# Second feed-forward products of phases one and two as seven block products, sums kept in DRAM

## The chip, the cores and the metric

The kernel runs on one core of one Trainium2 chip. The metric is the device time of one execution in microseconds (us). Three runs of the kernel before gave 1245.04, 1245.33 and 1245.99 us, median 1245.33.

## What is computed

A decoder trunk of two layers on 512 tokens of width 1024, all float32. Each layer is a mixer (layer 0: gated linear recurrence and retention; layer 1: sparse attention) and a SwiGLU feed-forward part of hidden width 2816, both behind an RMS norm and added to the residual:

```
def swiglu(x, w1, w3, w2):
    return (jax.nn.silu(x @ w1) * (x @ w3)) @ w2
...
for layer in range(DEPTH):
    hn = rmsnorm(h, attn_norm[layer])
    ...
    h = h + swiglu(rmsnorm(h, ffn_norm[layer]), ffn_w1[layer], ffn_w3[layer], ffn_w2[layer])
return rmsnorm(h, final_norm)
```

The change is in the feed-forward part, which runs once per layer, so twice.

## The kernel before, in words

Each float32 product is made of three passes at the fast matmul rate: an operand is split into a rounded high part and the rest (`mm3`, lines 196 to 203: high by high on L201, then the two mixed passes on L202 and L203). Weights come from DRAM in pieces of at most 1 MB into one of four `wr` buffers (SyncE's queue, L117). ScalarE casts a half of such a piece into `whi` (L136, two instructions), and VectorE makes `wlo` (L137). `prefetch` (L180) keeps this at most four parts of 1024 columns ahead of the matmuls; `whi` and `wlo` have four buffers each.

The residual `h` is held feature-major: two tiles of 128 partitions by 4 by 512 tokens. The feed-forward part (`ffn`, L702) walks the hidden width in three phases `ph` of 1024, 1024 and 768 columns. A phase has two first products, `q` = 0 and 1 (512 hidden columns each, 384 in the third phase), and then the second product:

- A first product gives w1 and w3 at once by `strassen` (L275): seven block products instead of eight, called here by their place `j` = 0 to 6 and by the PSUM tile they use (X, Y, V, V, X, X, Z). Each has 2 row blocks by 4 terms by 3 passes, 24 matmuls. The weight operands that are sums of blocks are formed by DMA: `plan_set` (L151) loads three blocks and adds others onto them with an accumulating DMA issued by GpSimd (L161), eight of them per set of weights. `keep` (L284) copies a PSUM result to an SBUF tile `part`, `add` (L288) adds a later one to it. The result is token-major (tokens on partitions). SiLU and the product with the other half follow (L735, L741), then four TensorE transposes per token block (`turn`, L723, L726) and the split into `gh` and `gl` (L729, L730), feature-major.
- The second product takes w2 as weights and `gh`, `gl` as the moving side (L761 to L801): eight output blocks `m` of 128 features, each with 8 terms by 3 passes of 512 columns in phases one and two. `done` (L765) adds the PSUM tile to `h` (L767). Its weights are plain loads, four pieces of 1 MB a phase (`w2a`, `w2c`), each split once.

Every engine runs its own queue in order. The instructions of a queue are ordered ahead of time from the program text and priorities, and semaphores do the rest. GpSimd's queue holds the accumulating DMAs in this part of the program, SyncE's queue the plain DMAs. Pools: `big` has 13 buffers of 8 KB per partition (seven hold the first products' operands, two `h`, four `gh` and `gl`), `gr` 12 buffers of 2 KB.

Of the kernel before, what the change touches and what calls it, by code (L numbers as in the profile page):

```python
# [17 lines left out]
F32 = mybir.dt.float32  # L18
# [45 lines left out]
class Trunk:  # L64
# [210 lines left out]
    def strassen(self, sg, n, after, last):  # L275
# [8 lines left out]
        def keep(b, name, i, r):  # L284
            c = rest[name, i] = self.g2([P, S], name="part")[:, 0:n]
            A.activation(c, ps[b, i][:, 0:n], AF.Copy, scale=r())

        def add(b, name, i, r):  # L288
            c = rest.pop((name, i))
            V.scalar_tensor_tensor(c, ps[b, i][:, 0:n], r(), c, op0=ALU.mult, op1=ALU.add)  # L290
            after(name, i, c)
        R = lambda t: (lambda: self.rtok[:, t:t + 1])
        N = lambda t: (lambda: self.ntok[:, t:t + 1])
        for j, (b, op) in enumerate((("X", "A11"), ("Y", "A12"), ("V", "S1"), ("V", "S4"), ("X", "S2"), ("X", "S3"), ("Z", "A22"))):
            last(j)
            if j == 1:
                for i in range(2):
                    keep("X", "11", i, R(i))
            first = j in (0, 1, 2, 6)
            for i in range(2):  # L300
                if first:
                    ps[b, i] = self.psA("ps_" + b) if b in "XV" else self.psB("ps_" + b)
                o = ps[b, i][:, 0:n]
                self.mm3(o, [self.sg_at(sg, op, p, slice(i * P, (i + 1) * P)) + w.at((j * 4 + p) * n, (j * 4 + p + 1) * n) for p in range(4)], first, True, j in (3, 4, 5))
                if j == 1:
                    add("Y", "11", i, R(i))
                elif j == 2:
                    keep("V", "22", i, R(2 + i))
                elif j == 3:
                    keep("V", "12", i, R(i))  # L310
                elif j == 4:
                    add("X", "12", i, N(i))
                elif j == 5:
                    add("X", "22", i, N(2 + i))
                    keep("X", "21", i, R(2 + i))
                elif j == 6:
                    add("Z", "21", i, R(2 + i))
# [366 lines left out]
    def plan_ffn(self, layer):  # L684
        for ph in range(3):
            for j in range(2):
                if ph < 2:
                    self.plan_set("wff%d" % layer, (2 * ph + j,), 2048)
                else:
                    self.plan_set("wfg%d" % layer, (j,), 1536)  # L690
            for j in range(2):
                if ph < 2:
                    self.plan("w2a%d" % layer, 2 * ph + j, 2048)
                else:
                    self.plan("w2b%d" % layer, j, 1536)
            for j in range(2):
                if ph < 2:
                    self.plan("w2c%d" % layer, 2 * ph + j, 2048)
                else:
                    self.plan("w2d%d" % layer, j, 1536, 768)  # L700

    def ffn(self, layer, sg, gain_next, want_hg=True):  # L702
# [10 lines left out]

        for ph in range(3):
            gs = []
            for q in range(2):
                n = S if ph < 2 else 3 * P
                nj = n // P
                g = [self.b8([P, 4, S], F32R, name="g" + x) for x in "hl"]
# [3 lines left out]
                def turn(t, v, g=g, nj=nj):  # L723
# [3 lines left out]
                    p4 = pt[:, 0:nj * P].rearrange("p (j c) -> p j c", j=nj)  # L727
                    hi, lo = (x[:, 0:nj, t * P:(t + 1) * P] for x in g)
# [15 lines left out]
                def before(j):  # L744
# [4 lines left out]
                    flush(j)  # L749

                flush(7)
                later[:] = [(j - 7, f) for j, f in later]
                self.strassen(sg, n, after, before)
# [20 lines left out]
            flush(7)  # L774
            w = [self.unit(), self.unit()]
# [36 lines left out]
        return hn  # L812

# [545 lines left out]
def pack(i):  # L1359
# [28 lines left out]
    for l in range(2):  # L1388
# [8 lines left out]
        o["w2a%d" % l] = c(np.stack([w2u((4 * q, 4 * q + 4), (0, 4)) for q in range(4)]))  # L1397
        o["w2b%d" % l] = c(np.stack([w2u((16 + 3 * q, 19 + 3 * q), (0, 4)) for q in range(2)]))
        o["w2c%d" % l] = c(np.stack([w2u((8 * ph, 8 * ph + 8), (4 + 2 * q, 6 + 2 * q)) for ph in range(2) for q in range(2)]))
# [28 lines left out]
```

## Time and profile before

| | |
|---|---|
| median of three runs | 1245.33 us |
| the profiled execution, time and span | 1245.73 us, 1243.8 us |
| TensorE matmul busy | 1221.5 us, 98% of the span |
| VectorE, ScalarE, GpSimd busy | 799.1, 686.3, 232.0 us |
| granted TensorE clock | 0.996 of full speed |
| the chain that ended last | PE 88%, ACT 5%, DVE 4% |
| DMA bytes | 149.23 MB, 120 GB/s on average |

A matmul's row shows about 0.39 us from its start to its modelled end, but the next starts after 0.23 us: what counts is the distance between starts. The same holds for short instructions on ScalarE and VectorE, whose starts follow each other some 0.1 us closer than the rows' durations say.

### The profile page before, as it was taken

What the parts mean: (1) busy time and instruction counts of PE and PEld (TensorE: products, weight loads), DVE (VectorE), ACT (ScalarE), POOL (GpSimd) and SP (SyncE); (2) the same over time, 40 slices, a digit from 0 to 9 for tenths busy, and PEclk for the clock granted to TensorE, in tenths of its full rate; (3) what the DMA queues carried; (4) which work ended last, traced back from release to release, by engine and by line L of the source; (5) the groups of instructions that cost most, each with busy time, mean ns of one, the idle gap of its engine ahead of it and who ended that gap; (6) DMA issues with size and microseconds to landing.
All of it is one profiled execution on the core that took longest, in us unless ns stands there. A gap on an engine that the chain in (4) does not pass through costs nothing.

```text
span 1243.8 us, 16442 instructions
## 1 busy us (share of the span) xinstructions
PE 1221.5 (98%) x6077; PEld 1031.4 (83%) x6077; DVE 799.1 (64%) x1237; ACT 686.3 (55%) x1395; POOL 232.0 (19%) x303
## 2 busy tenths in 40 slices
PE   9999999999999999999999999999999999999997
PEld 7688888888888889988888878877888888888996
DVE  6886629666356636674364889986776537653764
ACT  6541447664256426655454688995666336633653
POOL 0001420220012002100000568680111011101200
PEclk9999999999999999999999999999999999999998
DMA  9122143784388328852100000134488358824832
GB/s 342 68 102 68 35 169 102 172 191 150 98 191 178 138 64 182 228 194 71 66 35 1 1 1 1 35 113 159 108 197 186 120 120 185 201 82 106 181 93 68
DMA packets 35535, 149.23 MB, mean 120 GB/s; under 512 B 3936, under 2 KB 6256, under 8 KB 26624
## 3 DMA queue, kind: packets, MB, share of 16 engines
q1 hardware_dynamic: 21296, 100.88, 22.8%
q0 software_dynamic: 14016, 47.27, 21.4%
q8 instruction: 48, 0.79, 0.2%
q14 instruction: 31, 0.25, 0.1%
q10 hardware_dynamic: 144, 0.04, 0.0%
HBM read 143.98 MB, written 4.19 MB: 119 GB/s over the span
## 4 chain that ended last, share of the span: by engine, by line
PE 88%; ACT 5%; DVE 4%; POOL 1%; issue 1%; DMA 0%; POOLq 0%; DVEq 0%; SPq 0%; ACTq 0%
PE ps L203 6%; PE ps L201 6%; PE ps L202 6%; PE ps_t L201 5%; PE ps_X L201 5%; PE ps_X L203 5%; PE ps_X L202 5%; PE ps_t L203 5%; PE ps_t L202 5%; PE ps_V L201 3%; PE ps_V L203 3%; PE ps_V L202 3%; ACT prob L1175 2%; PE ps_Y L201 2%; PE ps_Z L203 2%; PE ps_Z L201 2%
## 5 line engine op out<-in xcount | busy, mean ns | idle before, releaser
L136 ACT CAST whi<-wr 128x512 fp32r<-128x512 f32 (+1 forms) x540 | 295.1, 593 | 348.1 <-PE ps L202 126.2
L137 DVE TENSOR_TENSOR wlo<-wr,whi 128x1024 fp32r<-128x1024 f32 (+2 forms) x272 | 313.3, 1154 | 208.9 <-ACT whi L136 205.4
L201 PE MATMUL ps<-gh,whi 128*128 128x512 f32 (+1 forms) x364 | 139.8, 384 | 0.0
L203 PE MATMUL ps<-gh,wlo 128*128 128x512 f32 (+1 forms) x364 | 139.2, 382 | 0.0
L202 PE MATMUL ps<-gl,whi 128*128 128x512 f32 (+1 forms) x364 | 139.1, 382 | 0.0
L161 POOL DMA_DIRECT2D wr<-wff x64 | 55.6, 868 | 366.8 <-DVE wlo L137 327.8
L201 PE MATMUL ps_t<-whi,hgh 128*128 128x512 f32 x288 | 114.7, 399 | 0.0
L202 PE MATMUL ps_t<-wlo,hgh 128*128 128x512 f32 x288 | 113.3, 394 | 0.0
L203 PE MATMUL ps_t<-whi,hgl 128*128 128x512 f32 x288 | 112.7, 391 | 0.0
L201 PE MATMUL ps_X<-whi,sg 128*128 128x512 f32 (+1 forms) x288 | 107.2, 372 | 0.0
L203 PE MATMUL ps_X<-whi,sg 128*128 128x512 f32 (+1 forms) x288 | 106.9, 371 | 0.0
L202 PE MATMUL ps_X<-wlo,sg 128*128 128x512 f32 (+1 forms) x288 | 106.8, 371 | 0.0
L1185 POOL TENSOR_TENSOR prob<-prob,rs 128x384 f32<-128x384 f32 (+3 forms) x128 | 88.1, 722 | 1.9
L767 DVE TENSOR_TENSOR h<-ps,h 128x512 f32<-128x512 f32 x46 | 31.8, 691 | 82.6 <-PE ps L203 82.6
L203 PEld LDWEIGHTS ps<-gh,wlo 128*128 128x128 f32 x364 | 68.4, 188 | 13.3
L202 PEld LDWEIGHTS ps<-gl,whi 128*128 128x128 f32 x364 | 68.4, 188 | 13.2
L201 PEld LDWEIGHTS ps<-gh,whi 128*128 128x128 f32 x364 | 68.4, 188 | 13.0
L1175 ACT ACTIVATE prob<-ps_s,nm 128x384 f32<-128x384 f32 (+3 forms) x128 | 68.2, 540 | 15.8 <-DVE nm L1171 14.9
L201 PE MATMUL ps_V<-whi,sg 128*128 128x512 f32 (+1 forms) x192 | 71.2, 371 | 0.0
L202 PE MATMUL ps_V<-wlo,sg 128*128 128x512 f32 (+1 forms) x192 | 71.2, 371 | 0.0
L203 PE MATMUL ps_V<-whi,sg 128*128 128x512 f32 (+1 forms) x192 | 71.2, 371 | 0.0
L203 PEld LDWEIGHTS ps_t<-whi,hgl 128*128 128x128 f32 x288 | 54.1, 188 | 11.5 <-issue 0.2
(316 smaller groups left out, 2568.6 us busy)
## 6 DMA issues: line engine op xcount, KB each, us to landing
wr<-wff POOLq DMA_DIRECT2D x64, 512.0 KB, 5.9
wr<-wff SPq DMA_DIRECT2D x24, 1024.0 KB, 4.8
wr<-wfg POOLq DMA_DIRECT2D x32, 384.0 KB, 5.8
wr<-w0t SPq DMA_DIRECT2D x10, 1024.0 KB, 5.9
wr<-w1t SPq DMA_DIRECT2D x10, 1024.0 KB, 4.9
wr<-wfg SPq DMA_DIRECT2D x12, 768.0 KB, 4.3
wr<-w2a SPq DMA_DIRECT2D x8, 1024.0 KB, 4.8
wr<-w2c SPq DMA_DIRECT2D x8, 1024.0 KB, 5.0
```

What stands on the lines that cost most here:

```text
L136: self.nc.scalar.copy(hi[:, c], x[:, c])
L137: self.nc.vector.tensor_tensor(lo, x, hi.bitcast(F32), op=ALU.subtract)
L161: self.nc.gpsimd.dma_start(x[:, c], more[:, c], accum_op=ALU.add)
L201: mm(ps, ah, bh, start=(first and k == 0), stop=False)
L202: mm(ps, ah, bl, start=False, stop=False)
L203: mm(ps, al, bh, start=False, stop=(last and k == n - 1))
L767: V.tensor_tensor(hm, ps, hm, op=ALU.add)
L1175: A.activation(u.p[:, r, b, 0:u.nk], u.ps[:, b, :], AF.Exp, bias=u.nm[:, b:b + 1], accum_out=u.rs[:, r, b:b + 1])
L1185: Q.tensor_tensor(x, x, u.rs[:, r, b:b + 1].broadcast_to([P, u.nk]), op=ALU.mult)
```

## The change

The second products of phases one and two now also go by `strassen`, with the hidden values as the stationary side and w2 as the moving side, so that their results are token-major. The first products of these phases leave the hidden values unsplit in one tile `g` each. A new function `second` forms from them the seven left operands `gop` (A11, A12, S1, S4, S2, S3, A22; four of them sums or differences of quarters, made in place on VectorE), each split into high part (ScalarE, L856 of the changed kernel) and rest (VectorE, L857), one product ahead of its use; two buffers of the pool `big` are left for them. `strassen` gets these operands through a function and without scale factors. w2 comes by `plan_set` as a set of four blocks `w2s`. Each finished sum of 128 tokens by 512 features is written to the DRAM tensor `sums` (L888). In the third phase the sum of phase one is read back (L775), that of phase two is added by an accumulating DMA (L776), and `turned` transposes it (four TensorE transposes of 128 by 128) and adds it to `h`; one of the eight sums is turned ahead of each of the block products 1 to 6 of the third phase's first first product, and 1 and 2 of its second. The third phase's own second product is unchanged.

```diff
@@ -272,7 +272,8 @@
         for i, w in ((0, u), (2, v)):
             put(*(sg[2][z][p // 2][:, p % 2, i:i + 2] for z in range(2)), w)
-    def strassen(self, sg, n, after, last):
+    def strassen(self, opnd, n, after, last, scaled=True):
         nc = self.nc
@@ -283,11 +284,17 @@
         def keep(b, name, i, r):
             c = rest[name, i] = self.g2([P, S], name="part")[:, 0:n]
-            A.activation(c, ps[b, i][:, 0:n], AF.Copy, scale=r())
-
-        def add(b, name, i, r):
+            if scaled:
+                A.activation(c, ps[b, i][:, 0:n], AF.Copy, scale=r())
+            else:
+                A.copy(c, ps[b, i][:, 0:n])
+        def add(b, name, i, r, sub=False):
             c = rest.pop((name, i))
-            V.scalar_tensor_tensor(c, ps[b, i][:, 0:n], r(), c, op0=ALU.mult, op1=ALU.add)
+            if scaled:
+                V.scalar_tensor_tensor(c, ps[b, i][:, 0:n], r(), c, op0=ALU.mult, op1=ALU.add)
+            else:
+                V.tensor_tensor(c, c, ps[b, i][:, 0:n], op=ALU.subtract if sub else ALU.add)
             after(name, i, c)
         R = lambda t: (lambda: self.rtok[:, t:t + 1])
         N = lambda t: (lambda: self.ntok[:, t:t + 1])
@@ -301,7 +308,7 @@
                 if first:
                     ps[b, i] = self.psA("ps_" + b) if b in "XV" else self.psB("ps_" + b)
                 o = ps[b, i][:, 0:n]
-                self.mm3(o, [self.sg_at(sg, op, p, slice(i * P, (i + 1) * P)) + w.at((j * 4 + p) * n, (j * 4 + p + 1) * n) for p in range(4)], first, True, j in (3, 4, 5))
+                self.mm3(o, [opnd(op, p, slice(i * P, (i + 1) * P)) + w.at((j * 4 + p) * n, (j * 4 + p + 1) * n) for p in range(4)], first, True, j in (3, 4, 5))
                 if j == 1:
                     add("Y", "11", i, R(i))
                 elif j == 2:
@@ -309,9 +316,9 @@
                 elif j == 3:
                     keep("V", "12", i, R(i))
                 elif j == 4:
-                    add("X", "12", i, N(i))
+                    add("X", "12", i, N(i), True)
                 elif j == 5:
-                    add("X", "22", i, N(2 + i))
+                    add("X", "22", i, N(2 + i), True)
                     keep("X", "21", i, R(2 + i))
                 elif j == 6:
                     add("Z", "21", i, R(2 + i))
@@ -688,16 +695,13 @@
                     self.plan_set("wff%d" % layer, (2 * ph + j,), 2048)
                 else:
                     self.plan_set("wfg%d" % layer, (j,), 1536)
+            if ph < 2:
+                self.plan_set("w2s%d" % layer, (ph,), 2048)
+                continue
             for j in range(2):
-                if ph < 2:
-                    self.plan("w2a%d" % layer, 2 * ph + j, 2048)
-                else:
-                    self.plan("w2b%d" % layer, j, 1536)
+                self.plan("w2b%d" % layer, j, 1536)
             for j in range(2):
-                if ph < 2:
-                    self.plan("w2c%d" % layer, 2 * ph + j, 2048)
-                else:
-                    self.plan("w2d%d" % layer, j, 1536, 768)
+                self.plan("w2d%d" % layer, j, 1536, 768)
     def ffn(self, layer, sg, gain_next, want_hg=True):
         nc = self.nc
@@ -711,12 +715,24 @@
             while later and later[0][0] <= j:
                 later.pop(0)[1]()
+        sums = self.dram.tile([2, NT, P, D], F32, name="sums%d" % layer)
+        back = []
+        def turned(t, c, tiles):
+            pt = self.psC("ps_tr")
+            for k in range(4):
+                T.transpose(pt[:, k * P:(k + 1) * P], tiles[:, k * P:(k + 1) * P], self.ident)
+            x = h[c][:, :, t * P:(t + 1) * P]
+            V.tensor_tensor(x, pt.rearrange("p (k s) -> p k s", k=4), x, op=ALU.add)
         for ph in range(3):
             gs = []
             for q in range(2):
                 n = S if ph < 2 else 3 * P
                 nj = n // P
-                g = [self.b8([P, 4, S], F32R, name="g" + x) for x in "hl"]
+                g = [self.b8([P, 4, S], F32R, name="g" + x) for x in "hl"] if ph == 2 else self.b8([P, 4, S], name="g")
                 gs.append((g, nj))
                 vals = {}
@@ -725,6 +741,9 @@
                     for j in range(nj):
                         T.transpose(pt[:, j * P:(j + 1) * P], v[:, j * P:(j + 1) * P], self.ident)
                     p4 = pt[:, 0:nj * P].rearrange("p (j c) -> p j c", j=nj)
+                    if nj == 4:
+                        A.copy(g[:, :, t * P:(t + 1) * P], p4)
+                        return
                     hi, lo = (x[:, 0:nj, t * P:(t + 1) * P] for x in g)
                     A.copy(hi, p4)
                     V.tensor_tensor(lo, p4, hi.bitcast(F32), op=ALU.subtract)
@@ -747,10 +766,19 @@
                         self.ntok = self.const.tile([P, NT], F32, tag="ntok", name="ntok", bufs=2)
                         V.tensor_scalar(self.ntok, self.rtok, -1.0, None, op0=ALU.mult)
                     flush(j)
+                    if j and back:
+                        turned(*back.pop(0))
+                    if ph == 2 and q == 0:
+                        for i in range(j + (j > 0), j + 2):
+                            x = self.g2([P, S], name="sum")
+                            src = [sums[u, i // 2, :, i % 2 * S:(i % 2 + 1) * S] for u in range(2)]
+                            nc.sync.dma_start(x, src[0])
+                            nc.gpsimd.dma_start(x, src[1], accum_op=ALU.add)
+                            back.append((i // 2, i % 2, x))
                 flush(7)
                 later[:] = [(j - 7, f) for j, f in later]
-                self.strassen(sg, n, after, before)
+                self.strassen(partial(self.sg_at, sg), n, after, before)
             if ph == 2 and want_hg:
                 self.load_gates()
                 hn = self.new_hg()
@@ -772,6 +800,9 @@
                     if not want_hg:
                         A.activation(hm, hm, AF.Copy, scale=self.gain[4][:, m:m + 1])
             flush(7)
+            if ph < 2:
+                self.second(gs[0][0], gs[1][0], sums[ph], flush)
+                continue
             w = [self.unit(), self.unit()]
             ps = [self.psA("ps_2") for _ in range(4)]
             nj = [gs[q][1] for q in range(2)]
@@ -810,6 +841,54 @@
         for _ in late:
             pass
         return hn
+    def second(self, g0, g1, dst, flush):
+        V, A = self.nc.vector, self.nc.scalar
+        a, b = slice(0, 256), slice(256, S)
+        src = {"A11": g0[:, :, a], "A12": g1[:, :, a], "S3": g0[:, :, b], "A22": g1[:, :, b], "S2": g0[:, :, a], "S4": g1[:, :, a]}
+        ops = {}
+        def make(n):
+            t = ops[n] = self.b8([P, 2, 4, 256], F32R, name="gop")
+            for c in (slice(0, 2), slice(2, 4)):
+                x = src[n][0 if c.start == 0 else 1] if n == "S1" else src[n][:, c]
+                A.copy(t[:, 0, c], x)
+                V.tensor_tensor(t[:, 1, c], x, t[:, 0, c].bitcast(F32), op=ALU.subtract)
+        def sums1():
+            src["S1"] = []
+            for c in (slice(0, 2), slice(2, 4)):
+                x = self.g2([P, 2, 256], name="s1")
+                V.tensor_tensor(x, g0[:, c, b], g1[:, c, b], op=ALU.subtract)
+                src["S1"].append(x)
+        def sums2():
+            for z, c in enumerate((slice(0, 2), slice(2, 4))):
+                V.tensor_tensor(g0[:, c, b], g0[:, c, a], g0[:, c, b], op=ALU.subtract)
+                V.tensor_tensor(g0[:, c, a], src["S1"][z], g0[:, c, a], op=ALU.subtract)
+                V.tensor_tensor(g1[:, c, a], g1[:, c, a], g0[:, c, a], op=ALU.add)
+        def before(j):
+            if j == 0:
+                make("A12")
+            elif j == 1:
+                flush(99)
+                sums1()
+                make("S1")
+                sums2()
+            elif j < 6:
+                make(("S4", "S2", "S3", "A22")[j - 2])
+        def after(name, i, c):
+            t = 2 * (name[0] == "2") + i
+            u = name[1] == "2"
+            self.nc.sync.dma_start(dst[t, :, u * S:(u + 1) * S], c)
+        make("A11")
+        self.strassen(lambda n, p, c: tuple(ops[n][:, z, p, c] for z in range(2)), S, after, before, False)
     def rope(self, x, n, cos, sin):
@@ -1394,9 +1473,10 @@
         t2 = w2.reshape(NH, P, 8, P)
         w2u = lambda j, m: t2[slice(*j)][:, :, slice(*m)].transpose(1, 2, 0, 3).reshape(P, -1)
-        o["w2a%d" % l] = c(np.stack([w2u((4 * q, 4 * q + 4), (0, 4)) for q in range(4)]))
+        half = lambda ph, z, u: w2[1024 * ph + 512 * z:1024 * ph + 512 * z + 512, 512 * u:512 * u + 512].reshape(4, P, 512).transpose(1, 0, 2).reshape(P, -1)
+        o["w2s%d" % l] = c(np.stack([np.stack([half(ph, z, u) for u in range(2) for z in range(2)]) for ph in range(2)]))
         o["w2b%d" % l] = c(np.stack([w2u((16 + 3 * q, 19 + 3 * q), (0, 4)) for q in range(2)]))
-        o["w2c%d" % l] = c(np.stack([w2u((8 * ph, 8 * ph + 8), (4 + 2 * q, 6 + 2 * q)) for ph in range(2) for q in range(2)]))
         o["w2d%d" % l] = c(np.stack([w2u((16, 22), (4 + 2 * q, 6 + 2 * q)) for q in range(2)]))
     w = i["nsa_w_in"][0]
     o["w1t"] = tm(np.concatenate([w[:, 1024:2560].reshape(D, 3, 512).reshape(D, -1), w[:, :1024]], axis=1))
```

The order on GpSimd's queue, the accumulating DMAs of layer 0's feed-forward part. `wr` is the raw weight buffer, `wff`, `wfg` and `w2s` are weights in DRAM, `sum` is an SBUF tile and `sums` the DRAM tensor. Before:

```order
L658 TENSOR_TENSOR rs<-va,mhalf 128x8
L659 TENSOR_TENSOR tok_q<-tok_q,rs 128x512
L570 TENSOR_TENSOR y<-y,xc 128x512 x4
L668 TENSOR_TENSOR tok_g<-tok_g,tok_q 128x512 x4
L161 DMA wr<-wff 128x1024 x2
L345 TENSOR_TENSOR rtok<-ms,mhalf 128x4
L161 DMA wr<-wff 128x1024 x30
L161 DMA wr<-wfg 128x768 x16
```

Now:

```order
L161 DMA wr<-wff 128x1024 x14
L161 DMA wr<-w2s 128x1024 x8
L161 DMA wr<-wff 128x1024 x16
L161 DMA wr<-w2s 128x1024 x8
L161 DMA wr<-wfg 128x768 x2
L776 DMA sum<-sums_1813 128x512 x3
L161 DMA wr<-wfg 128x768 x2
L776 DMA sum<-sums_1813 128x512
L161 DMA wr<-wfg 128x768 x4
L776 DMA sum<-sums_1813 128x512 x3
L161 DMA wr<-wfg 128x768 x2
L776 DMA sum<-sums_1813 128x512
```

Sixteen accumulating DMAs for w2 have come in, and the eight that bring the sums stand between those of the third phase's weights.

VectorE's queue in phase one's second product. Before, from the end of the first product's last block (`part` are first products' results):

```order
L290 SCALAR_TENSOR_TENSOR part<-ps_Z,rtok,part 128x512
L137 TENSOR_TENSOR wlo<-wr,whi 128x1024
L741 TENSOR_TENSOR part<-part 128x512
L137 TENSOR_TENSOR wlo<-wr,whi 128x1024
L730 TENSOR_TENSOR gl<-ps_tr,gh 128x4x128 x2
L137 TENSOR_TENSOR wlo<-wr,whi 128x1024
L767 TENSOR_TENSOR h<-ps_2479,h 128x512
```

Now, from S1 (`s`) to the low half of operand S4 (the `gop` of the last row):

```order
L864 TENSOR_TENSOR s_2533<-g 128x512
L864 TENSOR_TENSOR s_2535<-g 128x512
L137 TENSOR_TENSOR wlo<-wr,whi 128x1024
L857 TENSOR_TENSOR gop<-s_2533,gop 128x512
L857 TENSOR_TENSOR gop<-s_2535,gop 128x512
L870 TENSOR_TENSOR g<-g 128x2x256 x2
L137 TENSOR_TENSOR wlo<-wr,whi 128x1024
...
L872 TENSOR_TENSOR g<-g 128x2x256 x2
L297 TENSOR_TENSOR part<-part,ps_Y 128x512
L137 TENSOR_TENSOR wlo<-wr,whi 128x1024
L297 TENSOR_TENSOR part<-part,ps_Y 128x512
L137 TENSOR_TENSOR wlo<-wr,whi 128x1024
L857 TENSOR_TENSOR gop<-g,gop 128x512 x2
```

Where the rows left out are the two of L871, thirteen short instructions and four of L137 stand from the first of these rows to the first half of S4's low part.

## Rows read from the trace of the kernel before

**Rows 1.** The profile page: busy time by engine.

```profile
PE 1221.5 (98%) x6077; PEld 1031.4 (83%) x6077; DVE 799.1 (64%) x1237; ACT 686.3 (55%) x1395; POOL 232.0 (19%) x303
```

**Rows 2.** Busy time by stretch, layer 0 feed-forward: engines, TensorE clock, DMA share, GB/s.

```profile
215.36:249.01 33.65, 33.65 (x153) 27.80 (x152) 22.39 (x29) 21.44 (x38) 7.13 (x7) 1.00 0.70 160
...
295.00:338.50 43.50, 43.50 (x197) 36.12 (x196) 18.64 (x21) 10.50 (x19) 1.73 (x2) 1.00 0.40 111
...
418.30:461.90 43.60, 43.60 (x198) 36.18 (x198) 17.88 (x21) 9.89 (x19) 1.73 (x2) 1.00 0.28 80
461.90:493.00 31.10, 31.10 (x180) 30.58 (x179) 19.15 (x26) 19.28 (x42) 6.92 (x8) 1.00 0.74 161
493.00:523.00 30.00, 30.00 (x178) 29.64 (x177) 20.16 (x29) 19.86 (x43) 5.76 (x7) 1.00 0.87 201
```

**Rows 3.** Timeline of TensorE (start, us, engine, line): first and after-last matmul of block product 0.

```profile
215.36 0.39 PE L201 MATMUL ps_X<-whi,sg 128*128 128x512 f32 x1
...
220.80 0.95 PE L340 MATMUL ps_stat<-ones,acc 128*128 128x1 f32 x8
```

**Rows 4.** Timeline of TensorE: two matmuls of 384 columns; four transposes between matmuls.

```profile
485.03 0.33 PE L202 MATMUL ps_X<-wlo,sg 128*128 128x384 f32 x1
485.20 0.33 PE L203 MATMUL ps_X<-whi,sg 128*128 128x384 f32 x1
...
589.70 0.66 PE L936 MATMUL ps_tr<-ident,kv 128*128 128x128 f32 x4
590.11 0.47 PE L201 MATMUL ps_t<-whi,hgh 128*128 128x512 f32 x1
590.43 0.39 PE L202 MATMUL ps_t<-wlo,hgh 128*128 128x512 f32 x1
```

**Rows 5.** Timeline of VectorE: two short ones, and a weight split with the next instruction.

```profile
292.66 1.29 DVE L730 TENSOR_TENSOR gl<-ps_tr,gh 128x512 fp32r<-128x512 f32 x2 [0.35 <-ACT gh L729]
...
295.31 1.23 DVE L137 TENSOR_TENSOR wlo<-wr,whi 128x1024 fp32r<-128x1024 f32 x1
296.46 0.75 DVE L290 SCALAR_TENSOR_TENSOR part<-ps_Z,rtok,part 128x512 f32<-128x512 f32 x1
```

**Rows 6.** Timeline of ScalarE: two casts of a weight half, then a SiLU.

```profile
289.92 1.13 ACT L136 CAST whi<-wr 128x512 fp32r<-128x512 f32 x2
290.96 0.63 ACT L735 ACTIVATE part<-part 128x512 f32<-128x512 f32 x1
```

**Rows 7.** DMA queues, 215 to 295 us: packets, MB, share of 16 engines; q0 is GpSimd's.

```profile
q0 software_dynamic: 2016, 7.34, 49.9%
q1 hardware_dynamic: 921, 6.76, 24.6%
```

**Rows 8.** DMA, 222 to 240 us: queue share, and issue to landing (median us).

```profile
q0 software_dynamic: 737, 2.70, 80.6%
...
wr<-wff POOLq DMA_DIRECT2D x6, 512.0 KB, 7.8
```

**Rows 9.** DMA issues: at 274.10 and 448.86 us alone, and of the whole span (median landing).

```profile
wr<-wff POOLq DMA_DIRECT2D x1, 512.0 KB, 5.1
...
wr<-wfg POOLq DMA_DIRECT2D x1, 384.0 KB, 4.7
...
h<-hdram SPq DMA_DIRECT2D x8, 256.0 KB, 3.5
```

**Rows 10.** Timeline of GpSimd: two accumulating DMAs of 384 KB in a row.

```profile
468.55 0.86 POOL L161 DMA_DIRECT2D wr<-wfg  x1 [13.38 <-DVE wlo L137]
469.59 0.86 POOL L161 DMA_DIRECT2D wr<-wfg  x1 [0.18 <-issue]
```

**Rows 11.** Who waited for whom, 215 to 556 us: total, times, longest.

```profile
POOL wr L161 <- DVE wlo L137: 244.8, 40, 49.7
...
ACT whi L136 <- DMA wr<-wfg: 2.9, 4, 0.9
```

## The prediction

> **What bounds the kernel now.** Read the page first: TensorE is busy for 98% of the span [rows 1], so time goes where its stream of instructions gets shorter or has to wait. Then busy time by stretch for the feed-forward part [rows 2]: TensorE has no gap in any stretch and its clock stands at full speed; VectorE, at 18.6 of 43.5 us in a second product, has room. The last two columns matter most here: the DMA engines are busy 0.70 to 0.87 of the time beside first products, but only 0.40 and 0.28 beside the second products, which the change turns into the same kind of work. Third, the timeline of TensorE, for the price of one instruction by the distance of starts: block product 0 starts 24 matmuls at 215.36, and what follows starts at 220.80 [rows 3], so a matmul of 512 columns costs 5.44/24 = 0.227 us; one of 384 columns costs 0.17 [rows 4]. Last the DMA views: what a byte costs by queue [rows 7], and how long a transfer takes to land [rows 8, 9]. Today nobody waits for them: ScalarE's casts lost 2.9 us in four waits for accumulated weights [rows 11].
>
> **TensorE's own work.** A second product of phase one or two had 8 x 8 x 3 = 192 matmuls and gets 7 x 2 x 4 x 3 = 168. In two phases of two layers 96 matmuls go: 96 x 0.227 = 21.8 us less. Added are eight turned sums per layer, four transposes each. Four transposes start at 589.70, the next matmul 0.41 later, and the one after that 0.32 later instead of 0.227 [rows 4]: 0.50 us a sum, 16 x 0.50 = 8.0 us. The transposes of the hidden values are as many as before. Net: -13.8 us.
>
> **VectorE and ScalarE in the new second product.** VectorE gives 0.60 us to a short instruction (two take 1.29, one 0.69) and 1.15 to a weight split [rows 5]. Per second product it now has 14 splits (8 before), 14 low halves of operands, 8 sums and 8 PSUM additions: 14 x 1.15 + 30 x 0.60 = 34 us in 39. ScalarE casts a block of 512 columns every 0.52 us [rows 6]: 28 casts of weights, 14 of operands and 10 copies are 27 us. Both have room on the whole, and TensorE covers them, but operands are made only one product ahead. The tight place is S4, the fourth operand. Count from the start of block product 1, right behind the transposes of the last hidden values. ScalarE copies those out by about 1.1 (one cast and two copies). From there VectorE's queue, as printed above, runs 12 short instructions and 4 splits before S4's low half: 12 x 0.60 + 4 x 1.15 = 11.8, and 0.69 for its first half, done at 13.6. TensorE gets to S4 after two products, at 10.9, and does five matmuls that need high halves only, to 12.0. It waits 1.6 us, four times: +6.5 us. The trace has no such stall; its ends are 0 (queue counted a little too long) and 3 (a weight split more in front). I take 1.6, from rows. In the other products operands come 0.5 to 2 us early by the same count: no cost while VectorE's rows hold.
>
> **DMA.** In rows 7 GpSimd's accumulating queue took 49.9% of 80 us for 7.34 MB, 5.44 us per MB of all 16 engines; plain transfers 24.6% for 6.76 MB, 2.91 per MB. A set of weights is 3 plain loads and 8 accumulations of half a megabyte. Beside a changed second product stand a set (4.19 MB x 5.44 + 3.15 x 2.91 = 32.0 us) and the writing of eight sums (2.10 MB x 2.91 = 6.1): 38.1 us in 39, where 0.28 to 0.40 was. That is full but fits. In the third phase the two first products use 0.74 x 31.1 + 0.87 x 30.0 = 49.1 us of 61.1 [rows 2]. The sums add 2.10 MB read plain (6.1) and 2.10 MB accumulated (11.4): 66.6 us of demand in about 65. There is no slack left, and here TensorE waits by itself, since four transposes of a sum stand in its queue ahead of a block product.
>
> The first sum. Count from the start of Z, the last block product of phase two. SyncE's queue has its read behind the write of a sum that VectorE completes about 1.5 after; it lands 3 to 3.5 later [rows 9], at about 4.5 to 5. The accumulation lands 5.1 after issue for 512 KB and 4.7 for 384 KB when alone [rows 9], so about 4.3 for 256 KB (my estimate by that step): 8.8 to 9.3. TensorE wants it after Z and block product 0, 24 x 0.227 + 24 x 0.17 = 9.6. Alone it is just in time. But two accumulations of weights stand ahead on GpSimd (2.1 each), two sums are written and three read around it (0.8 each), and its own share is 1.4: 9.6 us of engine time begun some 2.3 after Z starts, 12 to 13 with a landing's end, and a weight load of 0.77 MB beside it. When six accumulations came close together, landing took 7.8 instead of 5.1 [rows 8, 9]. The wait is between 0 and 5.5; I take 4.0, since rows 8 (80% busy with that queue alone) are nearer to this stretch than a transfer alone.
>
> The fifth sum. Its accumulation stands behind the last pair of weight accumulations of that set, which wait for VectorE's splits (GpSimd spent most of the feed-forward part so: 244.8 us [rows 11]), and those for a weight buffer that block product 2 frees. From the end of block product 2: splits done by 2.1, the next issue 1.04 behind [rows 10], landing 4.3: 7.4, and TensorE asks after two products and two turned sums, 9.4. With the pair's 4.2 us of engine time ahead and plain transfers between, it lands at 10 to 14. Wait 0 to 5; I take 3.5.
>
> Both layers: 2 x (4.0 + 3.5) = +15 us. The other sums are asked for later and cost nothing while these two waits give the queues time to catch up. GpSimd's and SyncE's issuing itself is hidden; `done`'s additions to `h` (8 a phase) go, turned's come at the same price.
>
> **The sum.** -13.8 + 6.5 + 15 = +7.7. The profiled execution took 1245.73 us (1.9 of it around the span), 0.4 above the median: 1253.4 against it, 1253.0 against the median. A difference under 0.2%, 2.5 us, is about what a measurement of this kernel can't tell from none.
>
> **The rivals.**
> - **Transfers stay hidden, faster.** Both sums land within their slack in both layers, as a transfer alone does [rows 9]; it decides whether accumulations overlap more than rows 7 charge them. For it: today, at 0.87 busy, casts lose next to nothing [rows 11]. Against: rows 8. Then -13.8 + 6.5 = -7.3: 1238.0; without S4's wait 1231.5. The Trainium skill, page "DMA: Bandwidth & Descriptors", section "Anatomy of one DMA — SWDGE (gpsimd) path", fits a transfer from GpSimd by 2.0 us plus bytes over 436 GB/s; by that estimate a sum's accumulation lands in 2.6 us and this rival would hold. The trace disagrees for accumulations: 5.1 and 7.8 us where the fit says 3.2.
> - **Waits half as long, no change.** If each layer waits 3.7 in place of 7.5, -13.8 + 6.5 + 7.4 = 0: 1245.4.
> - **Weights late too, slower still.** A second product's DMA demand is 38.1 of 39 us; if accumulated weights of block products 5 and 6 come 1 to 2 us late because the writes of sums push them, four times 1.5 and a microsecond more per sum wait give 1253 + 6 + 4 = 1263. Against: the first products ran at 0.87 without it.
>
> **How the numbers follow.** Forecast 0.55, hidden transfers 0.25, half waits 0.13, late weights 0.07. Faster by over 0.2%: 0.25; within: 0.13; slower: 0.62. The forecast's own range, by the bounds of its waits, is 1248 to 1260. The range that should hold 8 in 10 takes in the half waits, the first rival's centre and part of the last: 1237 to 1262.
>
> **What would show it.** Right: matmuls at the same distance and 32 fewer instructions on TensorE; each changed second product about 39 to 41 us long; in the third phase two waits of TensorE for a tile `sum`, 3 to 5 us each per layer, DMA share near 1.0 there and accumulations landing after 7 us or more; one wait of 1 to 3 us at S4. Wrong: no wait of TensorE on `sum` (then the first rival), or waits on `wlo` in phases one and two (then the last), or a S4 wait of more than 3 us, which would put VectorE in the place of the bound.

## The result, and the profile after

The changed kernel takes 1261.51 us (median of four runs, 1257.42 to 1262.65), beside 1245.66 us for the kernel before: a ratio of 1.0124, 95% interval 1.0105 to 1.0142. It is 1.2% slower. The forecast was slower by 7.7 us; it is slower by 15.9, twice as much and at the upper end of the range. The profiled execution took 1262.65 us.

Of the page of the changed kernel, the span, the busy times, TensorE's granted clock in 40 slices and the chain that ended last:

```profile
span 1259.8 us, 16891 instructions
...
PE 1214.7 (96%) x6045; PEld 1023.9 (81%) x6045; DVE 866.7 (69%) x1333; ACT 756.6 (60%) x1531; POOL 273.4 (22%) x351
...
PEclk9999999999999989999999999998999999998999
...
PE 80%; ACT 6%; DVE 4%; issue 4%; DMA 3%; POOL 2%; SPq 0%; POOLq 0%; DVEq 0%; ACTq 0%
```

TensorE has the 32 instructions less that were counted and is busy 6.8 us less than before [rows 1], in a span that is 16.0 longer: it now waits. DMA has come into the chain that ended last with 3% (0% before). Busy time by stretch, the columns as in [rows 2]: phase one's second product, then two parts of the third phase's first products.

```profile
295.01:335.69 40.68, 39.38 (x177) 32.20 (x176) 34.21 (x44) 26.91 (x50) 6.91 (x8) 1.00 0.88 210
...
455.25:485.00 29.75, 22.78 (x123) 22.38 (x122) 12.78 (x17) 11.54 (x24) 11.03 (x13) 0.83 1.01 233
485.00:515.00 30.00, 27.30 (x166) 26.31 (x165) 20.80 (x32) 16.07 (x36) 6.42 (x8) 1.00 0.87 193
```

From the start of Z to the next first product TensorE took 49.98 us before (289.69 to 339.67) and now takes 46.22 (289.47 to 335.69), 3.76 less, where 24 matmuls are 5.44. VectorE works 34.2 us in it, as worked out (34), and the DMA engines are 0.88 busy. The first 30 us of the third phase hold what went wrong: TensorE is busy 22.8 of 29.75 us, its mean granted clock is 0.83, and the DMA engines have no idle share. Who waited for whom on TensorE, layer 0 in the first two lines, layer 1 in the third:

```profile
PE ps_tr L726 <- DMA sum<-sums: 9.6, 2, 7.0
PE ps_V L201 <- ACT part L290: 2.6, 2, 1.3
...
PE ps_tr L726 <- DMA sum<-sums: 8.2, 2, 6.9
```

The waits on `sum` are the two per layer that were named, the first and the fifth, but 7.0 and 2.6 us (6.9 and 1.3 in layer 1) in place of 4.0 and 3.5. TensorE's timeline around the first sum, layer 0:

```profile
459.27 0.34 PE L203 MATMUL ps_X<-whi,sg 128*128 128x384 f32 x1
466.58 1.08 PE L726 MATMUL ps_tr<-ident,sum 128*128 128x128 f32 x4 [6.97 <-DMA sum<-sums]
467.31 0.67 PE L201 MATMUL ps_Y<-whi,sg 128*128 128x384 f32 x1
467.78 0.52 PE L202 MATMUL ps_Y<-wlo,sg 128*128 128x384 f32 x1
468.10 0.52 PE L203 MATMUL ps_Y<-whi,sg 128*128 128x384 f32 x1
...
473.50 0.34 PE L203 MATMUL ps_Y<-whi,sg 128*128 128x384 f32 x1
473.68 0.60 PE L726 MATMUL ps_tr<-ident,sum 128*128 128x128 f32 x4
474.03 0.42 PE L201 MATMUL ps_V<-whi,sg 128*128 128x384 f32 x1
474.29 0.34 PE L202 MATMUL ps_V<-wlo,sg 128*128 128x384 f32 x1
...
478.28 0.60 PE L726 MATMUL ps_tr<-ident,sum 128*128 128x128 f32 x4
```

After the wait the matmuls start 0.32 us apart (467.78 to 468.10) where 0.174 is usual: the clock stands at the lower of its two levels, 1.2 GHz (the trace shows a granted clock of 0.50 from 466.58 to 470.00). A sum's transposes and a block product take 7.10 us here (466.58 to 473.68) and 4.60 the next time (473.68 to 478.28), so the lower clock cost another 2.5 us; in layer 1 it was 1.7. A turned sum by itself costs 0.44: the first matmul behind it starts 0.53 after the last one ahead (0.36 more than usual) and the second 0.26 after that (0.09 more).

How the first sum got so late: SyncE's read, and GpSimd's issues.

```profile
451.61 0.38 SPq L775 DMA_DIRECT2D sum<-sums x1
```

```profile
450.87 0.86 POOL L161 DMA_DIRECT2D wr<-wfg  x1 [13.69 <-DVE wlo L137]
452.33 0.86 POOL L161 DMA_DIRECT2D wr<-wfg  x1 [0.60 <-DVE wlo L137]
459.14 0.86 POOL L776 DMA_DIRECT2D sum<-sums  x1 [5.94 <-DMA sum<-sums]
```

The read was issued at 451.6, 1.8 us after Z started (449.81), as counted. It landed 7.5 us after the start of its issue, not 3 to 3.5; the accumulation, issued then, took 7.4, not 4.3 (7.0 and 7.3 by the DMA view, from which [rows 9] are). Right around the read stand two accumulations of weights, issued 0.7 us ahead of it and 0.7 behind.

### The profile page after: what moved, and what is told of

The parts are those of the page before. It is cut to its first block, busy times and chain, and to the rows that moved or that the text cites. A ratio compares the mean times of both kernels' runs of the same rounds, so it can differ in the third digit from the quotient of the medians.

```text
span 1259.8 us, 16891 instructions
## 1 busy us (share of the span) xinstructions
PE 1214.7 (96%) x6045; PEld 1023.9 (81%) x6045; DVE 866.7 (69%) x1333; ACT 756.6 (60%) x1531; POOL 273.4 (22%) x351
## 4 chain that ended last, share of the span: by engine, by line
PE 80%; ACT 6%; DVE 4%; issue 4%; DMA 3%; POOL 2%; SPq 0%; POOLq 0%; DVEq 0%; ACTq 0%
PE ps_X L201 6%; PE ps_X L203 6%; PE ps_X L202 6%; PE ps_t L201 5%; PE ps_t L203 5%; PE ps_t L202 5%; PE ps_V L201 4%; PE ps_V L203 4%; PE ps_V L202 4%; DMA sum<-sums 2%; PE ps_Y L201 2%; PE ps_Y L202 2%; PE ps_Y L203 2%; PE ps L201 2%; PE ps L203 2%
## 5 line engine op out<-in xcount | busy, mean ns | idle before, releaser
L136 ACT CAST whi<-wr 128x512 fp32r<-128x512 f32 (+1 forms) x588 | 322.5, 596 | 278.4 <-PE ps_t L203 51.3
L137 DVE TENSOR_TENSOR wlo<-wr,whi 128x1024 fp32r<-128x1024 f32 (+1 forms) x296 | 341.8, 1158 | 204.9 <-ACT whi L136 192.1
L201 PEld LDWEIGHTS ps_t<-whi,hgh 128*128 128x128 f32 x288 | 54.1, 188 | 11.5 <-ACT tok_v L522 0.6
L202 PEld LDWEIGHTS ps_t<-wlo,hgh 128*128 128x128 f32 x288 | 54.2, 188 | 10.6 <-issue 0.5
L1250 DVE TENSOR_REDUCE nm<-ps_s 128x1 f32<-128x384 f32 (+3 forms) x96 | 56.7, 594 | 7.4 <-PE ps_s L1246 6.3
L202 PEld LDWEIGHTS ps_X<-wlo,sg 128*128 128x128 f32 x288 | 54.1, 188 | 7.5
L203 PEld LDWEIGHTS ps_X<-whi,sg 128*128 128x128 f32 x288 | 54.1, 188 | 7.5
L201 PEld LDWEIGHTS ps_X<-whi,sg 128*128 128x128 f32 x288 | 54.1, 188 | 7.5
L1276 DVE TENSOR_TENSOR ptl<-ps_tr,pth 128x512 fp32r<-128x512 f32 x80 | 54.3, 679 | 7.1 <-ACT pth L1273 5.9
```

The costliest lines, as they stand in the source:

```text
L136: self.nc.scalar.copy(hi[:, c], x[:, c])
L137: self.nc.vector.tensor_tensor(lo, x, hi.bitcast(F32), op=ALU.subtract)
L201: mm(ps, ah, bh, start=(first and k == 0), stop=False)
L202: mm(ps, ah, bl, start=False, stop=False)
L203: mm(ps, al, bh, start=False, stop=(last and k == n - 1))
L1250: V.tensor_reduce(u.nm[:, 0:u.n], u.ps, axis=AX.X, op=ALU.max, negate=True)
```

## The experiments

Each ratio is to the kernel before on the same chip; the changed kernel's is 1.0124.

**Each sum turned two block products later** (the fifth and sixth, by this edit, three).

```diff
-                    if j and back:
+                    if j > (2 if q == 0 else 0) and back:
```

> Each sum is turned two block products later; reads, accumulations and their order on the queues stay. Latency theory: the chain of read and accumulation of the first sum ends some 7 us after TensorE asks for it, and the engines as a whole have room. Asked for two block products of 384 columns later (2 x 24 x 0.174 = 8.4 us), no sum is waited for, and the clock doesn't fall: 1261.5 minus 13.9 (first sums), minus 3.9 (fifth sums), minus about 4.8 (half clock behind the first wait) = 1239. Capacity theory (as in the prediction: 66.6 us of demand in 65): the engines are full, so the wait moves on to later sums or to the weights: 1250 to 1258.

Measured: 1254.81 us, 1.0059 (1.0043 to 1.0076). No sum is waited for now. TensorE stands 7.2 us per layer at another place, behind ScalarE, which waits for weights:

```profile
474.14 0.92 ACT L136 CAST whi<-wr 128x384 fp32r<-128x384 f32 x2 [7.43 <-DMA wr<-wfg]
```

```profile
460.16 0.86 POOL L776 DMA_DIRECT2D sum<-sums  x1 [6.71 <-DMA sum<-sums]
...
464.46 2.11 POOL L161 DMA_DIRECT2D wr<-wfg  x2
```

The latency theory is out as the whole cause: given time for the sums, the lateness moves to the weights. But the weights' second pair also stands behind the first sum on GpSimd's queue, so this run doesn't tell a full set of engines from a queue's order.

**Only two sums a layer.**

```diff
-                        for i in range(j + (j > 0), j + 2):
+                        for i in range(j + (j > 0), min(j + 2, 2)):
```

> Of each layer's eight sums only the first two are read back, accumulated and turned; the other six are left out (read, accumulation, transposes, addition to h). Crowding theory: the first sum is late because six more reads, a weight load and accumulations share the engines with it; without the later reads its read lands after about 4 us in place of 7.5 and its accumulation after 5 in place of 7.4, the wait shrinks from 7 to 1 or 2 us, and the clock stays up: 1261.5 - 12 x 0.5 (transposes) - 3.9 (fifth sums) - 11 (first waits) - 4.8 (clock) = 1236. Own-chain theory: the first sum is late for what stands ahead of it (its write, two transfers in a row, the accumulations of weights), so the wait stays near 7 us: 1261.5 - 6 - 3.9 = 1252.

Measured: 1249.57 us, 1.0018 (1.0006 to 1.0030). This is nearer to the own-chain theory's 1252 than to 1236. The first sum is waited for 6.3 us in layer 0 and 5.4 in layer 1 all the same:

```profile
PE ps_tr L726 <- DMA sum<-sums: 6.3, 1, 6.3
```

The crowding theory as I had put it, by the six later reads, is out: they cost 0.7 to 1.5 us, and without them the first sum's read lands no sooner (7.2 us after its issue by the DMA view, 7.0 with them).

**No accumulation in the third phase's weights.** `plan_set` of `wfg` leaves the accumulating DMAs out, so these operands are single blocks in place of sums.

```diff
-                if more is not None:
+                if acc and more is not None:
...
-                    self.plan_set("wfg%d" % layer, (j,), 1536)
+                    self.plan_set("wfg%d" % layer, (j,), 1536, False)
```

> The changed kernel with the accumulating DMAs of the third phase's weights left out (their operands are then single blocks; all else stays). Theory 1: the weights' accumulations that share the engines with the first sum's read make it late (two of 384 KB, 2.1 us of all engines each, issued just around the read): without them the read lands in 4 to 5 us in place of 7.5, its accumulation in about 5, the first wait falls from 7 us to 0 to 2 and the fifth's goes: about 1241. Theory 2: what stands ahead on SyncE's own queue (writes of sums, 0.77 MB of weights) makes it late; the wait stays at 4 us or more: 1250 to 1256.

Measured: 1247.93 us (median of ten), 1.0014 (1.0002 to 1.0025), between the two theories. The profiled execution took 1241.62 us, as theory 1 said; the nine others lay between 1244.99 and 1252.28 at a lower mean clock (0.990 to 0.994, the profiled one 0.996). Only the profiled one has rows. In it the read and the wait of layer 0 are:

```profile
452.17 0.39 SPq L775 DMA_DIRECT2D sum<-sums x1
```

```profile
456.84 2.65 POOL L776 DMA_DIRECT2D sum<-sums  x3 [19.08 <-DMA sum<-sums]
```

```profile
PE ps_tr L726 <- DMA sum<-sums: 1.7, 1, 1.7
```

The read lands after 4.6 us in place of 7.5 (4.1 in place of 7.0 by the DMA view), with the writes, the weight load and the later reads still around it, and the wait falls from 7.0 to 1.7 (in layer 1 from 6.9 to 1.5). By this one execution it is the two accumulations of weights beside the read that made it late, and not what stands ahead of it on SyncE's queue. What held the nine others is not shown.

**One read a block product, and weights first.** Two kernels for the question that the first run left open. The first reads and accumulates one sum a block product and turns it three products after:

```diff
-                    if ph == 2 and q == 0:
-                        for i in range(j + (j > 0), j + 2):
+                    if ph == 2 and (q == 0 or j == 0):
+                        for i in (j + 7 * q,):
```

> The changed kernel with its sums read and accumulated one a block product (sum k at block product k, the eighth at the second first product's start) and turned three block products after. Burst theory: the stretch as a whole has room, only the three or more sums asked at once push the weights aside; spread out, neither sums nor weights are waited for: 1240 to 1245. Capacity theory: the two first products want more transfer time than they last, so the weights come late as in e2: 1250 to 1258.

Measured: 1252.11 us, 1.0046 (1.0031 to 1.0062), within the capacity theory's range; TensorE loses 4.5 us a layer behind ScalarE, which waits for weights, and behind that wait its clock is lower too, 0.50 from 477 to 480 us:

```profile
ACT whi L136 <- DMA wr<-wfg: 8.7, 5, 4.8
```

```profile
477.00:480.00 3.00, 3.00 (x12) 2.90 (x11) 1.00 (x2) 1.82 (x5) 2.48 (x3) 0.50 1.08 208
```

The second puts a sum's accumulation behind the weights' latest on GpSimd's queue, and turns each sum one block product later still:

```diff
-                            nc.gpsimd.dma_start(x, src[1], accum_op=ALU.add)
...
+                        self.after(nc.gpsimd.dma_start(x, more, accum_op=ALU.add), self.last_acc)
```

> As the kernel with one read a block product, but on GpSimd's queue the first sum's accumulation stands behind two pairs of the third phase's weights in place of one, the others as late, and each sum is turned one block product later. The bytes are the same. Queue theory: the weights came late there (ScalarE waited 8.7 us for them) because their accumulations stood behind a sum's that waited for its read; now the second pair is issued as soon as VectorE's splits allow, ScalarE's waits for weights and the waits and half clock of TensorE behind them go (2 x 4.5 and 2 x 2 us): 1238 to 1242. Sharing theory: the engines hold more than the stretch can carry whatever the order, so weights or sums are still waited for: 1248 to 1254.

Measured: 1246.70 us, 1.0007 (0.9997 to 1.0017), between the two theories. GpSimd now waits for VectorE's splits alone, but ScalarE still waits for weights, more often and shorter:

```profile
ACT whi L136 <- DMA wr<-wfg: 10.4, 8, 2.3
```

The new order, with the turns one product later, was worth 5 us. That the rest comes from the sharing of the engines, which this profile shows 1.05 busy on average from 455 to 475 us, is argued and not shown: the fastest kernel below has its engines as full there and loses nothing.

**S4's operand earlier.** The same products with other intermediate sums:

```diff
+        def sums0():
+            for c in half:
+                V.tensor_tensor(g0[:, c, b], g0[:, c, a], g0[:, c, b], op=ALU.subtract)
...
+                V.scalar_tensor_tensor(x, g0[:, c, b], -1.0, g1[:, c, b], op0=ALU.mult, op1=ALU.subtract)
...
+                V.tensor_tensor(g0[:, c, a], src["S2"][z], g0[:, c, a], op=ALU.add)
...
+                V.tensor_tensor(g1[:, c, a], g1[:, c, a], src["S2"][z], op=ALU.add)
```

> The left operands are formed by another order of the same kind of sums (S3 ahead of the last hidden values, S2 = -S3 - A22, S1 = S2 + A11, S4 = A12 + S2), which takes two short instructions of VectorE (1.2 us) from in front of S4's low half. Theory 1, by my count: VectorE's low half sets the end of the 1.5 us wait at S4, so 4 x 1.2 = 4.8 us go: 1256.7, or less if S1 then comes late. Theory 2: ScalarE's copy of the PSUM tile, which stands behind four casts of weights, sets it; the wait stays near 1.3 us: 1260 to 1261.5.

Measured: 1258.39 us, 1.0089 (1.0069 to 1.0108), by the ratios 4.4 us less than the changed kernel. The stall itself is gone. First TensorE, ScalarE and VectorE of the changed kernel at S4, then TensorE here (first matmul of S1, the one that still waits a little, and the first behind S4):

```profile
306.81 0.39 PE L201 MATMUL ps_V<-whi,gop 128*128 128x512 f32 x1
...
312.48 0.39 PE L202 MATMUL ps_V<-wlo,gop 128*128 128x512 f32 x1
314.17 0.50 PE L201 MATMUL ps_V<-whi,gop 128*128 128x512 f32 x1 [1.30 <-ACT part L290]
...
315.03 0.39 PE L203 MATMUL ps_V<-whi,gop 128*128 128x512 f32 x1
...
319.60 0.39 PE L202 MATMUL ps_X<-wlo,gop 128*128 128x512 f32 x1
```

```profile
311.26 2.38 ACT L136 CAST whi<-wr 128x512 fp32r<-128x512 f32 x4
313.54 0.58 ACT L290 COPY part<-ps_V 128x512 f32<-128x512 f32 x1
```

```profile
314.04 1.28 DVE L857 TENSOR_TENSOR gop<-g,gop 128x512 fp32r<-128x512 f32 x2
```

```profile
306.64 0.39 PE L201 MATMUL ps_V<-whi,gop 128*128 128x512 f32 x1
...
314.03 0.50 PE L203 MATMUL ps_V<-whi,gop 128*128 128x512 f32 x1
...
317.77 0.39 PE L201 MATMUL ps_X<-whi,gop 128*128 128x512 f32 x1
```

In the changed kernel 49 matmuls (one of them of the next product) took 12.79 us from 306.81 to 319.60, 1.68 more than 49 x 0.2267. Here 48 take 11.13, 0.25 more. By the trace two things ended the stall almost together: ScalarE's copy behind four casts (314.1) and VectorE's first low half (314.7). The copy stands behind four casts still, but with S4's operand ready sooner, TensorE's own order has changed too: it does all of the first row block before it asks for the tile that the copy frees. So theory 1 holds for the size, and theory 2 for the row that the profile names; neither engine was the bound alone.

**Accumulation straight onto the finished tile.** Phase two's sums stay in SBUF; the chain that a turn waits for has one transfer in place of a write, a read and an accumulation, and it starts in the second product.

```diff
+            if j >= 4 and back:
+                turned(*back.pop(0))
...
+            if ph == 0:
+                self.nc.sync.dma_start(d, c)
+            else:
+                self.nc.gpsimd.dma_start(c, d, accum_op=ALU.add)
+                back.append((t, int(u), c))
```

> Phase two's sums stay in SBUF: phase one's sum is added from DRAM onto the finished tile by one accumulating DMA, and the tile is turned from block product 4 of phase two's second product on, one a block product. Eight writes and eight reads a layer go (4.2 MB). Latency theory: each sum has 8 us or more from its accumulation's issue to its turn, so no wait and no fall of the clock: 1261.5 - 13.9 - 3.9 - 4.8 = 1239. Capacity theory: the accumulations now lie beside the second product's own set (32.0 + 11.4 = 43 us of transfers in 39), so weights or sums come late by 3 to 5 us a layer: 1245 to 1249.

Measured: 1243.64 us, 0.9967 (0.9956 to 0.9978), faster than the kernel before, but 5 us above the latency theory's number (1.6 of them are the kernel before's, which took 1247.27 on this chip). One wait for a DMA is left per layer: the first tile's transposes stand earlier in TensorE's order than I had written them, inside S4.

```profile
435.06 0.66 PE L726 MATMUL ps_tr<-ident,part 128*128 128x128 f32 x2 [2.84 <-DMA part<-sums]
```

```profile
432.00:438.00 6.00, 3.16 (x11) 2.46 (x10) 5.72 (x8) 2.52 (x5) 3.51 (x4) 0.69 0.97 146
438.00:444.00 6.00, 6.00 (x21) 4.74 (x20) 0.57 (x1) 2.15 (x4) 0.00 (x0) 0.74 1.07 203
```

Behind this wait of 2.8 us the clock was lower (0.69, then 0.74 on average over 6 us); behind the changed kernel's wait of 2.6 at the fifth sum it was not (1.00 from 485 to 515 us).

**Both together, and the first turn one product later.** The edits of the last two kernels; the second kernel has `j >= 5` for `j >= 4`.

> Accumulation straight onto phase two's finished tile (as in e4) together with the other order of operand sums (as in e6). If the waits are single events that can be taken away one by one: no wait at S4 (4 x 1.5 us), TensorE comes to the first turned sum only when its tile has landed, and the clock stays up; what is left is the instruction count, -21.8 + 8.0 = -13.8: about 1231 to 1233. Rival, capacity: the engines are full from the second half of the second product to the middle of the third phase, so accumulated weights or sums come late by 3 to 5 us a layer all the same: 1238 to 1242.

> As e7, but the first sum is turned ahead of block product 5 of phase two's second product in place of 4, so each sum has 5.4 us more. If a landing a little too late is all that is left in e7, this one has none: 1231 to 1233, and e7 is 1 to 6 us above it. If the tiles held longer make ScalarE wait for a buffer, it is slower than e7.

Measured: 1232.67 us, 0.9890 (0.9875 to 0.9905), and 1232.40 us, 0.9888 (0.9874 to 0.9903). Both are 1.1% faster than the kernel before, and there is nothing between them: with S4 mended, the first turn stands where it was written and waits for nothing, at 436.88 us in the first kernel, ahead of block product 4, and in the second ahead of block product 5:

```profile
442.12 0.60 PE L726 MATMUL ps_tr<-ident,part 128*128 128x128 f32 x4
442.47 0.48 PE L201 MATMUL ps_X<-whi,gop 128*128 128x512 f32 x1
```

This is all that the count of instructions promised: 1246.59 on this chip less 13.8 is 1232.8. The second kernel's waits of TensorE in layer 0, and the stretch that holds the changed kernel's first wait and its low clock (7.0 + 2.5 us):

```profile
PE ps_X L201 <- DVE part L295: 0.6, 2, 0.4
```

```profile
455.00:465.00 10.00, 10.00 (x62) 9.93 (x61) 6.55 (x10) 4.93 (x11) 3.03 (x4) 1.00 1.08 242
465.00:475.00 10.00, 10.00 (x63) 9.93 (x62) 6.23 (x8) 5.83 (x12) 3.04 (x4) 1.00 1.07 190
```

The DMA engines are as full here as in the changed kernel, and TensorE waits for no DMA; ScalarE's casts wait 1.1 us for weights from 450 to 480 us.

**No sum through DRAM at all.** Both phases' tiles are turned directly, from block product 3 of either second product on.

```diff
-                    if ph == 2 and back:
+                    if back:
...
-            if j >= 5 and back:
+            if j >= 3 and back:
...
-            if ph == 0:
-                self.nc.sync.dma_start(d, c)
-            else:
-                self.nc.gpsimd.dma_start(c, d, accum_op=ALU.add)
-                back.append((t, int(u), c))
+            back.append((t, int(u), c))
```

> As e7b, but no sum goes through DRAM: phase one's sums are turned and added to h in phase two's first products too, so 32 sums are turned in place of 16 and the transfers of sums are gone. If a turned sum costs TensorE 0.44 us, as measured behind undisturbed block products, and e7b's transfers are hidden, this is 16 x 0.44 = 7 us above e7b: 1239 to 1240. If e7b still loses time to its transfers in places that no wait shows, the difference is smaller: 1233 to 1237.

Measured: 1238.97 us, 0.9941 (0.9925 to 0.9958): 6.6 us for 16 more turned sums, 0.41 each. The price of a turn holds, and in the faster kernel the transfers cost TensorE no time that these runs can tell.

## Why the prediction was right in direction and wrong in size

The direction, the two places and their engines were right; the size was off by a factor of two. Term by term, both layers, in us:

| term | forecast | measured |
|---|---|---|
| 96 matmuls less | -21.8 | -21.8 (24 still take 5.44) |
| 16 turned sums | +8.0 | +7.0 (0.44 each) |
| S4, four times | +6.5 | +6.7 (1.68 each) |
| first sum | +8.0 | +13.9 (7.0 and 6.9) |
| fifth sum | +7.0 | +3.9 (2.6 and 1.3) |
| lower clock behind the first wait | not in the sum | +4.2 (2.5 and 1.7) |
| sum | +7.7 | +13.9 |

The spans differ by 16.0. Of the 2.1 left, 1.4 lie between the two feed-forward parts (from 557.17 to 895.38 us before, 565.40 to 905.02 after), where the program is the same and where the kernels of this study took between 336.5 and 339.8 us; I don't explain it.

- **The step that failed is the first sum's wait**, put at 4.0 us a layer and measured at 7.0 and 6.9. It came from "9.6 us of engine time begun some 2.3 after Z starts, 12 to 13 with a landing's end". That prices the chain as engine time added up. But the accumulation can't start before the read has landed, and each of the two links took 3 to 4 us longer than its price: the read 7.5 us, issued between two accumulations of weights (4.6 in the one execution with rows that leaves them out), then the accumulation 7.4, landing 16.7 after Z started. [rows 8, 9] showed accumulations stretched from 5.1 to 7.8 where six came close together, and I applied no stretch to the read. The upper end given for this wait, 5.5, was too low as well.
- **The step that was missing is the clock.** The forecast charged a wait for its length only and put the time at the lower clock behind it at nothing, without a reason; it measured 2.5 and 1.7 us. Waits of the forecast's own size would not have been free of it: in the kernels with one read a block product and with weights first, waits of 4.5, 4.4, 3.1 and 2.9 us had matmuls at the lower clock behind them too, and behind that of 4.5 the next 36 matmuls and four transposes (474.86 to 484.22) took about 2.7 us more than at full speed.
- **The fifth sum** landed 12.0 us after the end of block product 2 in layer 0 and 10.7 in layer 1, within the 10 to 14 that were given, where 12.9 had been taken. What made the difference is not shown. It cancelled 3.1 of the 10.1 us that the first sums and the clock came out too low.
- **S4** came out as counted in size: 1.68 us for 1.6, with VectorE's first low half done 13.5 us after block product 1 began (301.25) where 13.6 was counted. What the profile names at the wait's end is ScalarE's copy, 0.6 us ahead of that low half, and the count had not named it. VectorE's work per second product was forecast as 34 us and is 34.2.
- **Slips of the working.** Four times 1.6 is 6.4, not 6.5. The forecast's own range, 1248 to 1260, does not follow from the bounds of its waits: 0 to 5.5 and 0 to 5 in two layers, on top of 1238, give 1238 to 1259. The landing of 5.1 that [rows 9] calls alone had another accumulation issued 1.4 us behind it (275.47).
- **The rivals.** "Transfers stay hidden" failed as the changed kernel stands. The Trainium skill's fit of a transfer from GpSimd (page "DMA: Bandwidth & Descriptors", section "Anatomy of one DMA — SWDGE (gpsimd) path") would give, as an estimate, 2.6 us for a sum's accumulation; here the first took 7.4, so by that fit the sum would have been taken for on time. "Waits half as long" failed: 8.9 us a layer on average, not 3.7. "Late weights" did not happen in the second products, at 0.88 of the engines; it happened in the third phase as soon as the sums were asked for later.

What stays open: how much of the weights' lateness in the kernels that turn later is GpSimd's order and how much the sharing of the engines. With one read a block product the time was 12.6 us above the count with S4's stall (1252.1 against 1246.6 - 13.8 + 6.7); weights first, turned one product later, gave back 5 of these. Open too is why nine of ten executions of the kernel without weight accumulations took 3 to 11 us more than the one that has rows; that these accumulations made the first read late rests on that one.

## What to carry to other kernels

Price a chain of dependent transfers link by link, each with the landing time that it has beside what else is in flight, not by its engine time added up. In the fastest kernel DMA engines as full (1.07 and 1.08) cost TensorE nothing, and the shortest chain (one accumulation onto a tile that is already there) gave a shorter time than every timing of the longer one. Where a wait of TensorE is forecast in the range of several us, add the time at the lower clock behind it as a term of its own; here it was 1.7 to 2.7 us behind waits of 4.5 to 7.0. An operand that is late by 1.5 us can cost more than that: in one kernel here the order of instructions had transposes in that gap, and these waited 2.8 us, longer than the operand did.

## What the runs showed that I had not expected

- Full DMA engines without a wait of TensorE for them: shares of 1.07 and 1.08 over 20 us in the fastest kernel, beside 1.01 over 30 us in the one that lost 9.5 us there (a share can read a little above 1).
- The later reads of 256 KB each, five of them issued before the first sum was turned or just behind, made the wait 1.5 us longer at most (5.4 or 6.3 without them, 6.9 or 7.0 with them); without two accumulations of 384 KB its read was 2.9 us shorter (4.6 for 7.5, in one profiled execution each).
- TensorE's clock was lower behind waits of 2.8 and 2.9 us in two kernels, and not behind one of 2.6 in another. The kernel without weight accumulations ran anywhere from 1241.6 to 1252.3 us with its clock at 0.996 down to 0.990.
